# Weight halves that start at changing offsets of 0 to 60 bytes in their buffers

## The chip, the core and the metric

The kernel runs on one core of a Trainium2 chip. The metric is the device time of one execution in microseconds (us). Engine names are those of the profile: PE is the matrix engine, PEld its weight loads, DVE the vector engine, ACT the scalar engine, POOL the general one, SP the queue that issues most DMAs.

## The reference, cut to what matters

Two decoder layers on 256 tokens of width 2048. Each layer projects the normalised input by one wide matrix, feeds four branches (a state-space scan, two attentions, a gated linear attention), projects each branch, gates and sums them, and projects the sum once more. All of it is float32.

```python
h = rmsnorm(x, pre_norm)
proj = h @ w_in                                  # 2048 x 20080 per layer
...                                              # four branches A, B, C, D
mixed = sum(gates[b] * (out[b] @ w_branch[b]) for b in "ABCD")
x = x + rmsnorm(mixed @ w_out, post_norm)
```

Weights are read once: 455 MB in all.

## The kernel before, in words

**Pieces of weight.** The weights are laid out on the host as pieces of 128 partitions x 1024 words (512 KB). `fetch` (L154 to L161) brings one piece: an SP DMA into a `raw` tile (five buffers), then ACT rounds it into `hi` (L158, an F32R tile, the matrix engine's rounded form of a 4-byte float), and DVE writes the rest `raw - hi` into `lo` (L159). `hi` and `lo` have three buffers each. 842 pieces go this way; six more, in the last stage of each layer, use buffers of their own (`own`, rows named `w_last`).

**Three products instead of one.** An activation is kept as two halves too (`hh`, `hl` in the tile `hx`; `oX_h`, `oX_l` of a branch X; `m_h`, `m_l`). A product is `hi*hh + lo*hh + hi*hl`.

- `chunk_a` (L165): the weight piece is the *moving* operand, 512 columns at a time; the activation is the stationary one, loaded anew for each matmul. A piece serves 12 matmuls of 512 columns (2 blocks of K, 2 halves of the tokens, 3 products), L179, L180, L181. 674 of the 842 pieces are used so.
- `chunk_b` (L186): the weight piece is the *stationary* operand, 128 columns at a time, and the activations move past it. A piece serves 8 loads of `hi` with 512 moving columns (L196, L200) and 8 loads of `lo` with 256 (L198). 144 pieces.
- `chunk_b4` (L213, 20 pieces) and the small projections (4 pieces of 896 words) also load the piece as stationary.

**Order.** The chunks run in a fixed order, layer by layer: acc_c, small, acc_lg, acc_uq/ur/uk/uv, acc_g, acc_gv, acc_gg, then for D, C, A and B a merge (acc_mX: gate, acc_bX: branch projection), between them acc_x, acc_z, acc_f, acc_fv, acc_fg, and acc_y last. The branch computations are generators that are stepped once per piece (`step`), so their instructions lie between the pieces' matmuls.

**Where the buffers lie.** In the built program the three `hi` buffers start 4096 bytes apart in each partition, the three `lo` buffers and the five `raw` buffers likewise, each on a multiple of 64 bytes. A matmul takes its columns from a `hi` or `lo` buffer from word 0 on in steps of 128, 256 or 512 words (112 words in the small projections), so every read of a piece starts on a multiple of 64 bytes.

Of the kernel before, what the change touches and what calls it, by code (L numbers as in the profile page):

```python
# [10 lines left out]
F32R = mybir.dt.float32r  # L11
# [7 lines left out]
P = 128  # L19
# [18 lines left out]
def trunk(ctx: ExitStack, tc: tile.TileContext, x, pos, vecs, rows, dskip, pre, post, glaw2,  # L38
# [5 lines left out]
    st = ctx.enter_context(tc.tile_pool(name="st", bufs=1))  # L44
# [96 lines left out]
    def step(n=1):  # L141
        for _ in range(n):
            while bg:
                try:
                    next(bg[0])
                    break
                except StopIteration:
                    bg.pop(0)

    def drain(gen=None):  # L150
        while bg and (gen is None or gen in bg):
            step()

    def fetch(src, n=1024, own=None):  # L154
        raw = st.tile([P, 1024], F32, tag="raw", name="raw", bufs=5)
        nc.sync.dma_start(raw[:, :n], src)
        hi, lo = own or (st.tile([P, 1024], F32R, tag=t, name=t, bufs=3) for t in ("hi", "lo"))
        S.copy(hi[:, :n], raw[:, :n])  # L158
        V.tensor_tensor(lo[:, :n], raw[:, :n], hi[:, :n].bitcast(F32), ALU.subtract)  # L159
        return hi, lo  # L160
# [4 lines left out]
    def chunk_a(src, p0, nk, xh, xl, k0, name, groups=None, own=None):  # L165

        acc = acc_tile(name)
        a2 = [acc[:, 0], acc[:, 1]]
        if own:
            a2[1] = ps.tile([P, 2, 512], F32, tag="s", name=name + "_1")[:, 0]  # L170
        kp = 0
        for n in groups or [1] * (nk // 2):
            w = [fetch(src[p0 + kp + i], own=own[i] if own and n > 1 else None) for i in range(n)]
            ks = [(2 * kp + i, w[i // 2], slice((i % 2) * 512, (i % 2 + 1) * 512)) for i in range(2 * n)]
            order = ([(tt, k) for k in ks for tt in range(2)] if n == 1 else
                     [(tt, k) for tt in range(2) for k in ks])
            for tt, (k, (hi, lo), c) in order:
                ts_ = slice(tt * P, (tt + 1) * P)
                PE.matmul(a2[tt], xh[:, k0 + k, ts_], hi[:, c], start=(k == 0), stop=False)  # L179
                PE.matmul(a2[tt], xh[:, k0 + k, ts_], lo[:, c], start=False, stop=False)  # L180
                PE.matmul(a2[tt], xl[:, k0 + k, ts_], hi[:, c], start=False, stop=(k == nk - 1))  # L181
            kp += n
            step(n)
        return a2 if own else acc

    def chunk_b(src, p0, name):  # L186

        acc = acc_tile(name)
        for b in range(2):
            for kh in range(2):  # L190
                hi, lo = fetch(src[p0 + 2 * b + kh])
                for k8 in range(8):
                    k = kh * 8 + k8
                    c = slice(k8 * P, (k8 + 1) * P)
                    if k < 15:
                        PE.matmul(acc[:, b], hi[:, c], hx[:, k].rearrange("p a t -> p (a t)"),  # L196
                                  start=(k == 0), stop=False)
                    PE.matmul(acc[:, b, 0:T], lo[:, c], hh[:, k], start=False, stop=False)  # L198
                    if k == 15:
                        PE.matmul(acc[:, b], hi[:, c], hx[:, k].rearrange("p a t -> p (a t)"),  # L200
                                  start=False, stop=True)
                step()
        return acc.rearrange("p b (a t) -> p b a t", a=2)
# [9 lines left out]
    def chunk_b4(src, p0, nb, xh, xl, k0, name):  # L213
        acc = acc_tile(name).rearrange("p a (b t) -> p (a b) t", t=T)
        for pp in range(nb // 2):
            hi, lo = fetch(src[p0 + pp])
            for j in range(2):
                b = 2 * pp + j
                for k in range(4):
                    c = slice((j * 4 + k) * P, (j * 4 + k + 1) * P)  # L220
                    PE.matmul(acc[:, b], hi[:, c], xh[:, k0 + k], start=(k == 0), stop=False)
                    PE.matmul(acc[:, b], hi[:, c], xl[:, k0 + k], start=False, stop=False)
                    PE.matmul(acc[:, b], lo[:, c], xh[:, k0 + k], start=False, stop=(k == 3))
            step()
        return acc
# [135 lines left out]
    for l in range(DEPTH):  # L361
# [27 lines left out]
        for kh in range(2):  # L389
            hi, lo = fetch(w_sm[l, kh], 896)  # L390
# [460 lines left out]
        for c in range(4):  # L851
            own = None
            if c == 3:
                own = sl.tile([P, 4, 1024], F32R, tag="mixed", name="w_last0")
                own2 = slot(7, "w_last1", F32R).rearrange("p (a n) -> p a n", a=2)
                own = [(own[:, 0], own[:, 1]), (own[:, 2], own[:, 3]), (own2[:, 0], own2[:, 1])]
# [114 lines left out]
```

## Time and profile before

| | |
|---|---|
| median of the runs | 2578.92 us (2578.37 to 2579.47, 2 runs) |
| profiled execution | 2579.64 us, its span 2577.6 us, so 2.0 us around the span |
| PE / PEld | 2546.1 / 2145.5 us busy (99% / 83%) |
| DVE / ACT | 1550.0 / 1259.8 us busy (60% / 49%) |
| HBM | 455 MB read, 178 GB/s over the span |
| granted clock of PE | 0.998 |

A row of the groups reads: line, engine, operation, out<-in, shapes, count | busy us, mean ns | idle time before it and what ended it. The ends of matmuls in the profile are modelled, so two rows of PE overlap (a mean of 390 ns where the next one starts 0.23 us later); the pace of PE is read from the starts.

### The profile page before, as it was taken

The numbers are of one execution on the slowest core, as the hardware profiler recorded it, in microseconds if no ns is written. First come the engines' busy times: TensorE is split into PE (matmuls) and PEld (weight loads), VectorE is DVE, ScalarE is ACT, GpSimd is POOL, SyncE is SP. The second block draws the span as 40 slices with busy tenths as digits, with TensorE's granted clock in tenths as the row PEclk, the third lists the DMA queues.
The fourth block names the chain that finished last, engine by engine and source line by source line (L and its number), as shares of the span: only waits on it lengthen the run. The fifth ranks groups of instructions, "written<-read, shape, count | busy, mean of one in ns | idle before, by whom it ended". The sixth has DMA issues, their size and how long they took to land.

```text
span 2577.6 us, 32544 instructions
## 1 busy us (share of the span) xinstructions
PE 2546.1 (99%) x12658; PEld 2145.5 (83%) x12658; DVE 1550.0 (60%) x1928; ACT 1259.8 (49%) x1625; POOL 25.6 (1%) x33
## 2 busy tenths in 40 slices
PE   8999999999999999999989999999999999999998
PEld 6898888888888888888878888888888888888887
DVE  6755855766655555555567568547665555565555
ACT  5554544555444444444455455445554454444443
POOL 0000000000000000000000000000000000000000
PEclk9999999999999999999999999999999999999999
DMA  6554555555555555665655445555555555556654
GB/s 227 182 164 147 168 168 183 185 180 171 193 183 180 172 172 186 206 189 180 211 163 187 156 146 168 171 185 187 176 172 191 188 177 173 173 172 204 189 180 155
DMA packets 126715, 461.34 MB, mean 179 GB/s; under 512 B 14657, under 2 KB 15169, under 8 KB 125665
## 3 DMA queue, kind: packets, MB, share of 16 engines
q1 hardware_dynamic: 126144, 459.11, 55.0%
q8 instruction: 99, 1.62, 0.3%
q14 instruction: 56, 0.45, 0.1%
q10 hardware_dynamic: 416, 0.17, 0.0%
HBM read 455.02 MB, written 4.19 MB: 178 GB/s over the span
## 4 chain that ended last, share of the span: by engine, by line
PE 98%; DVE 1%; ACT 1%; issue 0%; DMA 0%; POOL 0%; SPq 0%; DVEq 0%; POOLq 0%; ACTq 0%
PE acc_f L196 4%; PE acc_x L196 3%; PE acc_f L198 2%; PE acc_mC L180 2%; PE acc_mA L180 2%; PE acc_mA L179 2%; PE acc_mD L180 2%; PE acc_mC L179 2%; PE acc_mA L181 2%; PE acc_mD L179 2%; PE acc_mC L181 2%; PE acc_mD L181 2%; PE acc_mB L180 2%; PE acc_mB L179 2%; PE acc_mB L181 2%; PE acc_g L196 2%
## 5 line engine op out<-in xcount | busy, mean ns | idle before, releaser
L159 DVE TENSOR_TENSOR lo<-raw,hi 128x1024 fp32r<-128x1024 f32 x842 | 1027.9, 1223 | 796.1 <-ACT hi L158 793.7
L158 ACT CAST hi<-raw 128x1024 fp32r<-128x1024 f32 x842 | 883.4, 1050 | 1034.3 <-PE acc_mB L181 93.6
L196 PE MATMUL acc_f<-hx,hi 128*128 128x512 f32 x480 | 170.9, 397 | 0.0
L198 PE MATMUL acc_f<-hx,lo 128*128 128x256 f32 x512 | 139.7, 283 | 0.0
L196 PE MATMUL acc_x<-hx,hi 128*128 128x512 f32 x360 | 128.0, 396 | 0.0
L196 PEld LDWEIGHTS acc_f<-hx,hi 128*128 128x128 f32 x480 | 90.2, 188 | 20.1
L198 PE MATMUL acc_x<-hx,lo 128*128 128x256 f32 x384 | 105.0, 284 | 0.0
L180 PE MATMUL acc_mA<-lo,hx 128*128 128x512 f32 x256 | 103.7, 405 | 0.0
L180 PE MATMUL acc_mC<-lo,hx 128*128 128x512 f32 x256 | 102.7, 401 | 0.0
L180 PE MATMUL acc_mD<-lo,hx 128*128 128x512 f32 x256 | 102.4, 400 | 0.0
L179 PE MATMUL acc_mA<-hi,hx 128*128 128x512 f32 x256 | 101.6, 397 | 0.0
L181 PE MATMUL acc_mA<-hi,hx 128*128 128x512 f32 x256 | 100.5, 393 | 0.0
L179 PE MATMUL acc_mC<-hi,hx 128*128 128x512 f32 x256 | 100.3, 392 | 0.0
L180 PE MATMUL acc_mB<-lo,hx 128*128 128x512 f32 x256 | 100.2, 391 | 0.0
L179 PE MATMUL acc_mD<-hi,hx 128*128 128x512 f32 x256 | 99.9, 390 | 0.0
L181 PE MATMUL acc_mD<-hi,hx 128*128 128x512 f32 x256 | 99.8, 390 | 0.0
L181 PE MATMUL acc_mC<-hi,hx 128*128 128x512 f32 x256 | 99.7, 389 | 0.0
L181 PE MATMUL acc_mB<-hi,hx 128*128 128x512 f32 x256 | 99.7, 389 | 0.0
L179 PE MATMUL acc_mB<-hi,hx 128*128 128x512 f32 x256 | 99.6, 389 | 0.0
L198 PEld LDWEIGHTS acc_f<-hx,lo 128*128 128x128 f32 x512 | 96.6, 189 | 3.0
L181 PE MATMUL acc_y<-hi,m_l 128*128 128x512 f32 x232 | 91.5, 394 | 0.0
L180 PE MATMUL acc_y<-lo,m_h 128*128 128x512 f32 x232 | 90.4, 390 | 0.0
(422 smaller groups left out, 5637.7 us busy)
## 6 DMA issues: line engine op xcount, KB each, us to landing
raw<-in_w_in_dram SPq DMA_DIRECT2D x624, 512.0 KB, 3.4
raw<-in_w_br_dram SPq DMA_DIRECT2D x128, 512.0 KB, 3.4
raw<-in_w_out_dram SPq DMA_DIRECT2D x64, 512.0 KB, 4.0
raw<-in_w_ukv_dram SPq DMA_DIRECT2D x16, 512.0 KB, 4.3
raw<-in_w_uq_dram SPq DMA_DIRECT2D x12, 512.0 KB, 3.5
x<-in_x_dram SPq DMA_DIRECT2D x4, 512.0 KB, 5.6
xr<-in_x_dram SPq DMA_DIRECT2D x2, 1024.0 KB, 5.7
pn<-in_post_dram SPq DMA_DIRECT2D x2, 1024.0 KB, 5.5
```

What stands on the lines that cost most here:

```text
L158: S.copy(hi[:, :n], raw[:, :n])
L159: V.tensor_tensor(lo[:, :n], raw[:, :n], hi[:, :n].bitcast(F32), ALU.subtract)
L179: PE.matmul(a2[tt], xh[:, k0 + k, ts_], hi[:, c], start=(k == 0), stop=False)
L180: PE.matmul(a2[tt], xh[:, k0 + k, ts_], lo[:, c], start=False, stop=False)
L181: PE.matmul(a2[tt], xl[:, k0 + k, ts_], hi[:, c], start=False, stop=(k == nk - 1))
L196: PE.matmul(acc[:, b], hi[:, c], hx[:, k].rearrange("p a t -> p (a t)"), start=(k == 0), stop=False)
L198: PE.matmul(acc[:, b, 0:T], lo[:, c], hh[:, k], start=False, stop=False)
```

## The change

`fetch` takes `hi` and `lo` from buffers of 1040 words instead of 1024, and uses 1024 words of them that begin at word `i % 16` (for `hi`) and `(i + i // 16) % 16` (for `lo`), where `i` counts the pieces. So the start moves by 4 bytes from piece to piece, over 0 to 60 bytes, and the distance between the two starts changes every 16 pieces. The six pieces with buffers of their own stay as they were.

```diff
+    nth = [0]
+
     def fetch(src, n=1024, own=None):
         raw = st.tile([P, 1024], F32, tag="raw", name="raw", bufs=5)
         nc.sync.dma_start(raw[:, :n], src)
-        hi, lo = own or (st.tile([P, 1024], F32R, tag=t, name=t, bufs=3) for t in ("hi", "lo"))
+        if own:
+            hi, lo = own
+        else:
+            i = nth[0]
+            nth[0] += 1
+            hi, lo = (st.tile([P, 1040], F32R, tag=t, name=t, bufs=3)[:, o:o + 1024]
+                      for t, o in (("hi", i % 16), ("lo", (i + i // 16) % 16)))
         S.copy(hi[:, :n], raw[:, :n])
         V.tensor_tensor(lo[:, :n], raw[:, :n], hi[:, :n].bitcast(F32), ALU.subtract)
         return hi, lo
```

In the built program the instructions of every engine stand in the same order as before, row for row (11,670 rows on PE, 1,627 on DVE, 1,383 on ACT, 38 on POOL, 873 on SP), on the same buffers. What differs is addresses. The three `hi` buffers, and the three `lo` buffers, lie 4160 bytes apart instead of 4096, and all tiles behind them move up by a multiple of 64 bytes (384 bytes behind the last). Of the 8,088 matmuls with a piece as moving operand, 4,048 now start at an odd word and 6,060 at an address that is no multiple of 16 bytes; of the 2,880 loads of a piece as stationary operand, 1,432 and 2,160.

## The prediction

> **What bounds the kernel now.** I read the page's head first, then the chain that ended last, the groups, and the waits around `fetch`.
>
> ```profile
> span 2577.6 us, 32544 instructions
> PE 2546.1 (99%) x12658; PEld 2145.5 (83%) x12658; DVE 1550.0 (60%) x1928; ACT 1259.8 (49%) x1625; POOL 25.6 (1%) x33
> PE   8999999999999999999989999999999999999998
> PEclk9999999999999999999999999999999999999999
> PE 98%; DVE 1%; ACT 1%; issue 0%; DMA 0%; POOL 0%; SPq 0%; DVEq 0%; POOLq 0%; ACTq 0%
> ```
>
> PE is busy in every slice at full granted clock, and 98% of the chain is PE's own instructions, one after the other. So the time is the sum of PE's paces, and a change counts only if it alters the pace of a matmul or makes PE wait. Does PE wait for the split of a weight piece, the only code that the diff touches? The answers for the lines L159 and L158 list who waited for them:
>
> ```profile
>   ACT hi L158: 793.7, 619
>   PEld acc_c L180: 1.0, 2
>   PE acc_c L180: 0.4, 1
> ...
>   PEld acc_c L179: 3.5, 1
>   PE acc_c L179: 3.1, 1
> ```
>
> DVE waits 619 times for ACT's rounding (793.7 us), but PE waited for `lo` or `hi` only in acc_c, the first chunk, a few us in all. The split runs ahead. How far, and at what pace PE goes meanwhile, shows in the timeline of a merge stage:
>
> ```profile
> 1102.70 0.39 PE L180 MATMUL acc_mB<-lo,hx 128*128 128x512 f32 x1
> 1102.93 0.39 PE L181 MATMUL acc_mB<-hi,hx 128*128 128x512 f32 x1
> 1103.15 0.39 PE L179 MATMUL acc_mB<-hi,hx 128*128 128x512 f32 x1
> 1103.35 1.05 ACT L158 CAST hi<-raw 128x1024 fp32r<-128x1024 f32 x1 [1.66 <-PE acc_mB L181]
> 1103.38 0.39 PE L180 MATMUL acc_mB<-lo,hx 128*128 128x512 f32 x1
> 1103.61 0.39 PE L181 MATMUL acc_mB<-hi,hx 128*128 128x512 f32 x1
> ...
> 1104.44 1.22 DVE L159 TENSOR_TENSOR lo<-raw,hi 128x1024 fp32r<-128x1024 f32 x1 [1.49 <-ACT hi L158]
> ...
> 1105.65 0.39 PE L181 MATMUL acc_mB<-hi,hx 128*128 128x512 f32 x1
> ...
> 1106.07 1.05 ACT L158 CAST hi<-raw 128x1024 fp32r<-128x1024 f32 x1 [1.67 <-PE acc_mB L181]
> ```
>
> From the L181 at 1102.93 to the one at 1105.65 are 12 matmuls in 2.72 us: a start every 227 ns, 2.72 us per `chunk_a` piece. ACT begins a piece when PE frees its buffer (1103.35), DVE ends it at 1105.66, 2.31 us later; with three buffers PE still has two pieces to go, so it wants this one at about 1103.35 + 5.44 = 1108.8. The split is 3.1 us early, more than its own length.
>
> **The change part by part.** No instruction is added, removed or moved, and no wait is added: every engine's order is the same. SP's DMAs fill `raw`, which keeps its form. Four things read or write at new addresses.
>
> *1. ACT writes `hi`, DVE reads `hi` and writes `lo`, 842 times each, at 4 to 60 bytes past a 64-byte boundary in 15 of 16 cases.*
>
> ```profile
> L159 DVE TENSOR_TENSOR lo<-raw,hi 128x1024 fp32r<-128x1024 f32 x842 | 1027.9, 1223 | 796.1 <-ACT hi L158 793.7
> L158 ACT CAST hi<-raw 128x1024 fp32r<-128x1024 f32 x842 | 883.4, 1050 | 1034.3 <-PE acc_mB L181 93.6
> L690 DVE SCALAR_TENSOR_TENSOR xsT<-gt,vec,xsT x48: 475/479/482, 478.0 to 1797.0; 128x255 f32<-128x255 f32 x16, 128x254 f32<-128x254 f32 x16, 128x253 f32<-128x253 f32 x16
> L578 DVE TENSOR_SCALAR gla_x<-glz,vec x8: 475/478/484, 245.6 to 1531.2; 128x256 f32<-128x256 f32 x8
> ```
>
> The convolution (L690, `dst[:, j, i:]` with i of 1 to 3) already has DVE read and write at 4, 8 and 12 bytes: 479 ns for 253 to 255 elements, against 478 for 256 at an aligned place (L578). So DVE's price is 0, within 2 ns. For ACT no row shows such a write; DVE's 0 is the nearest, and the far end is a doubling. Neither end reaches PE alone: twice 1.05 us adds 1.05 to a chain that is 3.1 us early, and ACT's sum would go from 1260 to 2143 us of 2578. I take 0. Below 0 nothing is to be had, because PE does not wait there.
>
> *2. PE streams 8,088 matmuls of 512 columns (674 pieces x 12) from shifted places.* No row shows an F32R moving operand that starts off a 64-byte boundary, so I bound it by the nearest rows: DVE's 0 +/- 2 ns above, and the loads of L269, whose stationary operand `id2[:, 16 + h]` is F32R and starts at 4-byte steps (one word repeated):
>
> ```profile
> L269 PEld LDWEIGHTS S_B<-fR,id x32: 187/189/190, 690.6 to 2289.2; 128*128 128x128 f32 x32
> L198 PEld LDWEIGHTS acc_f<-hx,lo 128*128 128x128 f32 x512 | 96.6, 189 | 3.0
> L196 PEld LDWEIGHTS acc_f<-hx,hi 128*128 128x128 f32 x480 | 90.2, 188 | 20.1
> ```
>
> Across all 16 starts they take 187 to 190 ns, like the aligned loads of L196 and L198. So my value is 0 per matmul and the bounds are -2 and +2 ns: 8,088 x 2 ns = 16 us either way. Nothing covers this term: each ns per matmul is 8 us of time.
>
> [...]
>
> *3. PE loads 2,880 stationary blocks (144 pieces x 16 and the 20 + 4 others) from shifted places.* L269 says 0 +/- 2 ns. The loads run beside matmuls of the block before; uncovered, 2 ns each would be 6 us.
>
> *4. The tiles behind the buffers move by multiples of 64 bytes.* Their accesses keep their place within 64 bytes; I cost that at 0.
>
> Sum: 2579.6 (this execution) + 0, with -22 to +22. The profiled execution lies 0.7 us above the median, so the forecast is **2580 us**.
>
> **The rivals.**
>
> *A. The shift separates accesses that collide (faster).* Before, the buffers of one kind stand 4096 bytes apart, so ACT and DVE write at the offsets at which PE reads. If that cost PE time, matmuls beside a write should be slower, and stages should differ:
>
> ```profile
> L180 PE MATMUL acc_mA<-lo,hx 128*128 128x512 f32 x256 | 103.7, 405 | 0.0
> L180 PE MATMUL acc_mC<-lo,hx 128*128 128x512 f32 x256 | 102.7, 401 | 0.0
> L180 PE MATMUL acc_mD<-lo,hx 128*128 128x512 f32 x256 | 102.4, 400 | 0.0
> L179 PE MATMUL acc_mA<-hi,hx 128*128 128x512 f32 x256 | 101.6, 397 | 0.0
> L181 PE MATMUL acc_mA<-hi,hx 128*128 128x512 f32 x256 | 100.5, 393 | 0.0
> L179 PE MATMUL acc_mC<-hi,hx 128*128 128x512 f32 x256 | 100.3, 392 | 0.0
> L180 PE MATMUL acc_mB<-lo,hx 128*128 128x512 f32 x256 | 100.2, 391 | 0.0
> L179 PE MATMUL acc_mD<-hi,hx 128*128 128x512 f32 x256 | 99.9, 390 | 0.0
> L181 PE MATMUL acc_mD<-hi,hx 128*128 128x512 f32 x256 | 99.8, 390 | 0.0
> L181 PE MATMUL acc_mC<-hi,hx 128*128 128x512 f32 x256 | 99.7, 389 | 0.0
> L181 PE MATMUL acc_mB<-hi,hx 128*128 128x512 f32 x256 | 99.7, 389 | 0.0
> L179 PE MATMUL acc_mB<-hi,hx 128*128 128x512 f32 x256 | 99.6, 389 | 0.0
> ```
>
> The mean of the twelve is 393.8 ns, 4.8 above the lowest. If the whole excess were collisions, 8,088 x 4.8 = 39 us would go: 2541 us, still under 2%. But acc_mB, at the floor, has the same splits beside it as the others; it lacks branch work between its matmuls. And in the timeline the starts come 0.22 to 0.23 us apart whether a cast runs beside them (1103.38 to 1103.61) or neither engine writes (1102.70 to 1102.93). A whole collision relief is unlikely.
>
> *B. PE streams at half its pace from an odd word (slower).* The chain shows that this engine has two paces for 4-byte words: the F32R product of L179 and, beside it, the plain F32 scores of L272, with as many passes of 128 as of 256 columns:
>
> ```profile
> 149.35 0.23 PE acc_uv L179
> 149.58 1.97 PE S_D L272 x12
> ```
>
> 1.97 us / 12 = 164 ns for 192 columns on average, 0.855 ns a column; F32R goes at 227 / 512 = 0.443. If the fast pace needs words taken in pairs from an even place, the 4,048 matmuls that start at an odd word would take 512 x 0.855 = 438 ns, 211 more: 854 us, 3434 us in all. It decides the result from 52 us / 4,048 = 13 ns per odd matmul on. For it: the fast pace is twice the plain one, so something is widened. Against it: L269 and L690, which though repeat one word or take one at a time; no fast stream is among them. This is the rival I can least exclude.
>
> *C. The split itself slows and becomes the bound (slower).* If ACT and DVE both took twice as long off their boundaries, DVE's sum would be 1550 + 1028 = 2578 us, the whole span, and DVE's waits outside the split (2577.6 - 1550.0 - 796.1 = 231 us) would come on top in part: 2578 to 2809 us. It decides as soon as DVE's L159 is slower by some 80%. L690 speaks against it.
>
> **How the numbers follow.** The forecast (every pace within 2 ns) gets 0.80, the page's line penalty 0.05 (2591), rival A 0.04 (down to 2541), rival B 0.08 (3434, or a part of it), rival C 0.02; 0.01 for a gain beyond A. A measurement of this kernel tells about 2% from no change, 52 us. So faster 0.01, same 0.89, slower 0.10. The range takes the bounds of the forecast and the line penalty, which hold 0.85: 2560 to 2602 us. A part of A reaches into it.
>
> **What would show it.** Right: starts in acc_mB every 227 ns at every offset, L159 at 1223 ns and L158 at 1050, PE busy 99%, no wait of PE on `hi` or `lo` outside acc_c. [...] B: pieces alternate, every second one at up to 438 ns a matmul where `hi` starts odd, and acc_f, where pieces are stationary, changes otherwise. C: DVE near 100% and PE waiting for `lo`. What makes the prediction wrong is B first: a fast stream that no row here shows from an odd place.

## The result, and the profile after

The changed kernel takes 2614.44 us (median of 2614.19 to 2614.69) against 2578.92: a ratio of 1.0138, 95% interval 1.0094 to 1.0181. The profiled execution took 2614.69 us, its span is 35.0 us longer than before. The head of its page and its chain:

```profile
span 2612.6 us, 32544 instructions
PE 2580.4 (99%) x12658; PEld 2150.8 (82%) x12658; DVE 1551.8 (59%) x1928; ACT 1257.6 (48%) x1625; POOL 25.6 (1%) x33
PEclk9999999999999999999999999999999999999999
PE 97%; DVE 1%; ACT 1%; issue 0%; DMA 0%; POOL 0%; SPq 0%; DVEq 0%; POOLq 0%; ACTq 0%
```

PE's busy time grew by 34.3 us, so the time is PE's own; its granted clock is 0.997 against 0.998 before, and the waits on the split (DVE's `lo` at L167, ACT's `hi` at L166) are the same few in acc_c:

```profile
  PEld acc_c L188: 1.0, 2
  PE acc_c L188: 0.4, 1
...
  PEld acc_c L187: 3.7, 1
  PE acc_c L187: 3.3, 1
```

The groups say which matmuls (lines are 8 higher than before, 180 is now 188):

```profile
L167 DVE TENSOR_TENSOR lo<-raw,hi 128x1024 fp32r<-128x1024 f32 x842 | 1029.0, 1224 | 823.6 <-ACT hi L166 822.5
L166 ACT CAST hi<-raw 128x1024 fp32r<-128x1024 f32 x842 | 881.0, 1048 | 1070.1 <-PE acc_mB L189 97.9
L204 PE MATMUL acc_f<-hx,hi 128*128 128x512 f32 x480 | 170.4, 395 | 0.0
L206 PE MATMUL acc_f<-hx,lo 128*128 128x256 f32 x512 | 139.8, 283 | 0.0
L188 PE MATMUL acc_mB<-lo,hx 128*128 128x512 f32 x256 | 101.5, 396 | 0.0
L187 PE MATMUL acc_mB<-hi,hx 128*128 128x512 f32 x256 | 101.0, 395 | 0.0
L189 PE MATMUL acc_mB<-hi,hx 128*128 128x512 f32 x256 | 101.0, 395 | 0.0
```

Casts and subtractions are unchanged (1224 and 1048 ns against 1223 and 1050). `chunk_b`, where the piece is stationary, is unchanged (395 and 283 against 397 and 283; a pair of one matmul with `hi` and one with `lo` takes 350.6 ns from start to start in both). `chunk_a` is slower everywhere: the rows of acc_mB go from 389 to 391 up to 395 and 396. In the timeline of that stage:

```profile
1114.01 0.39 PE L189 MATMUL acc_mB<-hi,hx 128*128 128x512 f32 x1
1114.24 0.40 PE L187 MATMUL acc_mB<-hi,hx 128*128 128x512 f32 x1
1114.48 0.40 PE L188 MATMUL acc_mB<-lo,hx 128*128 128x512 f32 x1
...
1116.79 0.40 PE L189 MATMUL acc_mB<-hi,hx 128*128 128x512 f32 x1
```

From 1114.01 to 1116.79 are 12 starts: 232 ns each, against 227. Over all `chunk_a` matmuls that follow directly on one another, the mean distance of starts in the trace is 228.1 ns before and 232.7 after; 4.6 x 8,088 = 37 us, so these matmuls account for the whole loss of 35. Sorted by the word at which the moving half begins, the mean is 235 ns for words 1, 5, 9, 13, 233 for 2, 6, 10, 14, 231 for 3, 7, 11, 15, and 232 for 0, 4, 8, 12. So there is a saw-tooth over 16 bytes, and under it a rise that aligned starts pay too (232 at words 0, 4, 8, 12 against the 228.1 of before).

### The profile page after: what moved, and what is told of

It reads as the page before. It is cut to its first block, busy times and chain, and to the rows that moved or that the text cites. A ratio compares the mean times of both kernels' runs of the same rounds, so it can differ in the third digit from the quotient of the medians.

```text
span 2612.6 us, 32544 instructions
## 1 busy us (share of the span) xinstructions
PE 2580.4 (99%) x12658; PEld 2150.8 (82%) x12658; DVE 1551.8 (59%) x1928; ACT 1257.6 (48%) x1625; POOL 25.6 (1%) x33
## 4 chain that ended last, share of the span: by engine, by line
PE 97%; DVE 1%; ACT 1%; issue 0%; DMA 0%; POOL 0%; SPq 0%; DVEq 0%; POOLq 0%; ACTq 0%
PE acc_f L204 4%; PE acc_x L204 3%; PE acc_mC L188 2%; PE acc_mA L188 2%; PE acc_f L206 2%; PE acc_mD L188 2%; PE acc_mA L189 2%; PE acc_mA L187 2%; PE acc_mC L187 2%; PE acc_mD L187 2%; PE acc_mB L187 2%; PE acc_mB L189 2%; PE acc_mC L189 2%; PE acc_mB L188 2%; PE acc_mD L189 2%; PE acc_y L189 2%
## 5 line engine op out<-in xcount | busy, mean ns | idle before, releaser
L167 DVE TENSOR_TENSOR lo<-raw,hi 128x1024 fp32r<-128x1024 f32 x842 | 1029.0, 1224 | 823.6 <-ACT hi L166 822.5
L166 ACT CAST hi<-raw 128x1024 fp32r<-128x1024 f32 x842 | 881.0, 1048 | 1070.1 <-PE acc_mB L189 97.9
```

## The experiments

All times below are medians, beside runs of the kernel before on the same chip (2578.6 to 2579.5). "Pace" is the mean distance between the starts of `chunk_a` matmuls that follow directly on one another, worked out from the starts in the trace (distances over 270 ns, next to branch matmuls, are left out); acc_mB and acc_bB are the quietest stages, acc_mA has branch work between its matmuls.

| run | time, us | ratio (95%) | acc_mB | acc_bB | acc_mA |
|---|---|---|---|---|---|
| before | 2578.92 | | 226.9 | 226.7 | 229.3 |
| after | 2614.44 | 1.0138 (1.0094 to 1.0181) | 232.6 | 232.5 | 233.0 |
| pad_only | 2602.10 | 1.0089 (1.0074 to 1.0104) | 231.5 | 231.9 | 231.3 |
| const1 | 2649.27 | 1.0272 (1.0257 to 1.0287) | 237.5 | 237.7 | 237.2 |
| const3 | 2590.52 | 1.0044 (1.0029 to 1.0059) | 229.4 | 229.5 | 230.0 |
| lines | 2604.39 | 1.0098 (1.0081 to 1.0115) | 231.7 | 231.5 | 231.7 |
| both64 | 2590.42 | 1.0043 (1.0028 to 1.0058) | 229.0 | 228.9 | 230.0 |
| lo64 | 2608.39 | 1.0112 (1.0097 to 1.0127) | 231.9 | 232.0 | 231.9 |
| all64 | 2578.95 | 0.9999 (0.9989 to 1.0008) | 226.8 | 226.7 | 229.2 |
| hx15 | 2601.32 | 1.0084 (1.0069 to 1.0099) | 228.9 | 226.7 | 233.0 |
| sweep64 | 2600.31 | 1.0083 (1.0063 to 1.0104) | by chunk | | |
| sweep4 | 2611.28 | 1.0126 (1.0106 to 1.0146) | by chunk | | |
| sweep_lo | 2597.58 | 1.0073 (1.0053 to 1.0093) | by chunk | | |
| all4b | 2660.61 | 1.0316 (1.0299 to 1.0334) | 237.7 | 236.7 | 237.6 |
| frame | 2579.21 | 1.0000 (0.9991 to 1.0010) | 226.9 | 226.7 | 229.3 |
| word7 | 2572.95 | 0.9979 (0.9970 to 0.9988) | 227.2 | 227.2 | 227.5 |
| word7_b | 2573.07 | 0.9977 (0.9968 to 0.9987) | 227.2 | 227.2 | 227.5 |

### Place, mixing or spacing

Four kernels keep the 1040-word buffers and replace the two offsets of the change:

```diff
-                      for t, o in (("hi", i % 16), ("lo", (i + i // 16) % 16)))
+                      for t, o in (("hi", 0), ("lo", 0)))                              # pad_only
+                      for t, o in (("hi", 1), ("lo", 1)))                              # const1
+                      for t, o in (("hi", 3), ("lo", 3)))                              # const3
+                      for t, o in (("hi", 4 * (i % 4)), ("lo", 4 * ((i + i // 4) % 4))))  # lines
```

**pad_only**

> Buffers of 1040 words, every half begins at word 0. In the changed kernel a chunk_a matmul starts on average 4.3 ns later after the one before it, 35 us over 8,088 of them. Three theories. Place: it costs where a moving operand begins within 16 bytes (in the trace after, matmuls from words 1, 5, 9, 13 take about 235 ns to the next start, from 2, 6, 10, 14 about 233, from the others about 231). Mixing: it costs that neighbouring matmuls begin at different places, so that the even pace of 227 ns is lost. Spacing: it costs that the buffers stand 4160 bytes apart and other tiles moved. Place and mixing expect the time before, 2579 us; spacing expects about 2614.

**const1**

> All halves begin at word 1 of buffers of 1040 words. Place: the dearest place, without the aligned ones between; the one merge piece after the change with both halves at word 1 went at 238 ns a matmul against 227 before: 11 x 8,088 = 89 us, about 2668 us; at the least the 4 ns that separate words 1 and 0 in the trace after, 2611. Mixing: all starts are alike, so the even pace returns: 2579. Spacing: about 2614, as with word 0.

**const3**

> All halves begin at word 3 of buffers of 1040 words. Place: 228 to 230 ns a matmul, as in the merge pieces after the change with both halves at word 3, 7 or 15: 2587 to 2603 us, far below word 1 though the address is as odd. Mixing: 2579. Spacing: about 2614.

**lines**

> Starts change from piece to piece, but only by multiples of 16 bytes: word 4*(i%4) for hi and 4*((i+i//4)%4) for lo. [...] Mixing: neighbours still begin at different addresses, so the aligned matmuls pay what they pay in the trace after (231.5 ns against 228.1 before between such starts): 3.4 x 8,088 = 27 us, 2606. Spacing: about 2614.

Measured: pad_only loses 23 us with every start on a multiple of 64 bytes. That is 64% of the change's loss without its offsets, which "place" and "mixing" did not expect; "spacing" expected the whole. const1 is 47 us slower than pad_only, const3 12 us faster, so there is a place effect on top, and it is not oddness (237.5 ns at word 1, 229.4 at word 3 in acc_mB). The two parts do not simply add: at word 3 these buffers cost half of what they cost at word 0. "Mixing" falls with pad_only, const1 and const3, whose starts are all alike and which it put at 2579. lines does not decide against it: its 2604 us lie near the 2606 of "mixing", and 2 us above pad_only, so starts that change by multiples of 16 bytes cost next to nothing over the spacing.

Does the spacing act through ACT and DVE, which write beside PE? In acc_mB of pad_only the same 12 distances (ns) return whenever the same pair of buffers comes round. Two passes of one pair, worked out from the starts; A or D marks a distance of which ACT or DVE was busy for more than half:

```
231   240A  230A  234A  231A  232D  233D  240D  230D  234D  231D  232
231   240AD 230AD 234AD 231AD 232D  233D  240D  230D  234D  231D  232D
```

The pattern is the same, whatever the writers do (away from branch matmuls, over all passes, within 1 to 2 ns wherever a distance was seen with and without a writer). Over acc_mB and acc_bB the mean is 232.3 with neither busy, 231.3 with ACT, 231.7 with DVE, 231.1 with both. So no collision with the writers shows in these stages; what is left to look at is the addresses that PE itself reads, and the next runs move those.

### Which addresses

```diff
+            V.memset(st.tile([P, 16], F32, tag="gap_hi", name="gap_hi"), 0.0)   # both64: once, ahead of hi
             hi = st.tile([P, 1024], F32R, tag="hi", name="hi", bufs=3)
+            V.memset(st.tile([P, 16], F32, tag="gap_lo", name="gap_lo"), 0.0)   # lo64: once, ahead of lo
             lo = st.tile([P, 1024], F32R, tag="lo", name="lo", bufs=3)
+    V.memset(cp.tile([P, 16], F32, tag="gap_hx", name="gap_hx"), 0.0)           # all64: ahead of hx
-    hx = cp.tile([P, 16, 2, T], F32R, tag="hx", name="hx")                      # hx15, then rearranged to the four axes
+    hx = cp.tile([P, 16 * 2 * T + 16], F32R, tag="hx", name="hx")[:, 15:15 + 16 * 2 * T]
```

**both64**

> Buffers of 1024 words as before, 4096 bytes apart, but a gap of 64 bytes stands before the hi buffers, so all halves lie 64 bytes higher against the activations (hx, and the branch halves). Three theories for the 23 us that buffers of 1040 words cost with every start at word 0. Activations: PE's pace depends on where the moving half lies against the stationary block that is loaded for the next matmul; before, both are equal modulo 512 bytes, here they differ by 64: slower than 2579, towards the 2602 of the 1040-word buffers. Halves: it depends on where hi lies against lo (192 bytes apart modulo 512 in the 1040-word buffers, 0 here): 2579. Absolute: some addresses are slow in themselves: slower, like the first.

**lo64**

> As before, but a gap of 64 bytes between the hi and the lo buffers: hi stays equal to hx modulo 512 bytes, lo lies 64 higher. Activations: only the matmuls with lo (one in three) change their place against the stationary block: about a third of what all halves moved by 64 bytes cost. Halves: hi and lo differ in every piece: the full cost, towards 2602.

**all64**

> As before, but a gap of 64 bytes stands before hx, so that activations and halves all move up by 64 bytes together. Activations and halves: every relation is as before, 2579. Absolute: as slow as with the halves alone moved by 64 bytes.

**hx15**

> The activations hx begin at word 15 of a buffer that is 16 words longer; the halves of the weights start at word 0 of buffers of 1024 words. Seen from hx the halves lie 4 bytes further, as they did with all halves at word 1; the branch halves lie 64 bytes higher and keep their relation to the weights. If the dear places within 16 bytes (word 1) are places against the stationary block, the chunk_a stages with hx (acc_m, acc_gv, acc_fv and so on) go at 235 to 238 ns, as with all halves at word 1, and the time is near 2640. If they are places of the moving operand by itself, those stages go at 227 to 232 ns and only chunk_b, where hx moves, can change. acc_bX and acc_y, whose stationary blocks are not in hx, stay at 227 to 229 either way.

Measured: all64 returns to 2579 and to the paces of before, so 64 bytes more on every address cost nothing; only distances count at that step. both64 pays 11 us (229.0 ns in acc_mB against 226.9): the distance from the moving halves to the stationary blocks counts. lo64 pays 29 us, in all three products alike (232), though `hi` kept its distance to `hx`: the distance between `hi` and `lo`, which follow each other as moving operands, counts too, and more. Both theories of a distance hold in part; "a third of the cost" for lo64 was a miss.

hx15 was unclear on its own: the stages with `hx` go at 229 to 234, the branch stages as before, so there is a distance effect, but not the 237 of const1. In acc_mB the trace holds two even rhythms at the same distances, 226 and 227 ns in some stretches, 233 and 234 in others. The first chunk has both:

```profile
1074.54 0.39 PE L179 MATMUL acc_mB<-hi,hx 128*128 128x512 f32 x1
1079.98 0.40 PE L179 MATMUL acc_mB<-hi,hx 128*128 128x512 f32 x1
1080.21 1.04 PE L233 MATMUL tr_oB<-ident,fg 128*128 128x128 f32 x8
1081.32 0.39 PE L181 MATMUL acc_mB<-hi,hx 128*128 128x512 f32 x1
1097.41 0.40 PE L181 MATMUL acc_mB<-hi,hx 128*128 128x512 f32 x1
```

The first 24 distances are 226.7 ns on average, then eight branch matmuls come in, and the 69 distances from 1081.32 on are 233.2. The two last acc_mB chunks of the layer, with no branch matmul among theirs, keep 226.7 throughout. So one set of distances allows more than one pace (226.7 and 233.2 ns); in the first chunk the change stands at the branch matmuls.

### The law, by chunk

The sweeps use buffers of 1152 words (4608 bytes apart, equal modulo 512 again), four `raw` buffers instead of five to make room, and one offset per `chunk_a` chunk; everything else stays at word 0:

```diff
+        hi, lo = (st.tile([P, 1152], F32R, tag=t, name=t, bufs=3)[:, o:o + 1024]
+                  for t, o in (("hi", place[0]), ("lo", place[1])))
...
+        place[:] = 16 * (c % 8), 16 * (c % 8)                            # sweep64, c-th chunk_a
+        place[:] = (c + 4 * (c // 52)) % 16, (c + 4 * (c // 52)) % 16    # sweep4
+        place[:] = 0, 16 * (c % 8)                                       # sweep_lo
+        place[:] = 1, 1                                                  # all4b, with hx from word 1 of a longer buffer
```

**sweep64**

> Buffers of 1152 words (4608 bytes apart, equal modulo 512 as before; raw has four buffers instead of five). Every chunk_a chunk uses one distance for both halves, 64*(c mod 8) bytes for the c-th chunk, so the halves lie 0, 64, ... 448 bytes from the stationary blocks modulo 512 and equal to each other. Relation theory (the pace follows the distance between moving half and stationary block): the chunks at 0 go at 227 ns, those at 64 at 229 as in the run with all halves moved by 64 bytes, the others at paces of their own between 225 and 236, the same in both layers. If only the distance between hi and lo counts, all go at 227 to 229.

The timeline of sweep64, first and last start of an undisturbed row of matmuls in four neighbouring chunks, with both halves 256, 320, 384 and 448 bytes (0, 64, 128 and 192 modulo 256) from the stationary blocks; 95, 47, 95 and 47 distances lie between:

```profile
1139.83 0.39 PE L188 MATMUL acc_mB<-hi,hx 128*128 128x512 f32 x1
1161.40 0.39 PE L190 MATMUL acc_mB<-hi,hx 128*128 128x512 f32 x1
1161.63 0.40 PE L188 MATMUL acc_bB<-hi,oB_h 128*128 128x512 f32 x1
1172.40 0.39 PE L190 MATMUL acc_bB<-hi,oB_l 128*128 128x512 f32 x1
1172.63 0.40 PE L188 MATMUL acc_mB<-hi,hx 128*128 128x512 f32 x1
1194.72 0.39 PE L190 MATMUL acc_mB<-hi,hx 128*128 128x512 f32 x1
1194.95 0.39 PE L188 MATMUL acc_bB<-hi,oB_h 128*128 128x512 f32 x1
1205.91 0.40 PE L190 MATMUL acc_bB<-hi,oB_l 128*128 128x512 f32 x1
```

That is 227.1, 229.1, 232.5 and 233.2 ns. The chunks of the same stages one layer later, at 0, 64, 128 and 192, go at 227.1, 229.3, 232.5 and 233.2: the pattern repeats every 256 bytes.

**sweep_lo**

> The same buffers; hi stays at word 0, lo alone lies 64*(c mod 8) bytes higher. With lo 64 bytes higher in the earlier run every matmul took 232 ns, more than with both halves 64 higher (229). If the distance between hi and lo has its own price, the chunks at 0 go at 227 and all seven others at 230 to 234; if only the matmuls with lo pay by their distance to the stationary block, the chunk means lie a third of the way that the chunks with both halves moved go.

The same four distances for `lo` alone:

```profile
1137.58 0.39 PE L188 MATMUL acc_mB<-hi,hx 128*128 128x512 f32 x1
1159.16 0.39 PE L190 MATMUL acc_mB<-hi,hx 128*128 128x512 f32 x1
1159.38 0.39 PE L188 MATMUL acc_bB<-hi,oB_h 128*128 128x512 f32 x1
1170.29 0.40 PE L190 MATMUL acc_bB<-hi,oB_l 128*128 128x512 f32 x1
1170.53 0.39 PE L188 MATMUL acc_mB<-hi,hx 128*128 128x512 f32 x1
1192.68 0.39 PE L190 MATMUL acc_mB<-hi,hx 128*128 128x512 f32 x1
1192.91 0.40 PE L188 MATMUL acc_bB<-hi,oB_h 128*128 128x512 f32 x1
1203.68 0.39 PE L190 MATMUL acc_bB<-hi,oB_l 128*128 128x512 f32 x1
```

227.2, 232.1, 233.2 and 229.1 ns: at 64 bytes dearer than with both halves moved, at 192 cheaper. The distance between the halves has its own price (232.1 ns against 229.1 at 64 bytes). The expectation missed one thing: not all seven other distances are dear, since 256 bytes (227.2 ns) cost as little as 0 does in sweep64 (227.1). And the pace is not fixed by the distances alone: with `lo` 128 bytes (modulo 256) higher, undisturbed chunks of acc_lg and acc_y go at 231.1 ns, beside the 233.2 of acc_mB.

This also reads pad_only. There a third of the pieces have `hi` at distance 0 and `lo` 192 bytes higher (in the built program the three `hi` buffers lie 0, 64 and 128 bytes from `hx` modulo 256, the `lo` buffers 192, 0 and 64). Within such a piece of acc_bB the distances are 228 to 230 ns, as the 229.1 here, but for one of 240 after its first matmul, behind a piece of another buffer.

**sweep4**

> The same buffers, but both halves of a chunk begin at word 0, 1, ... 15, by chunk. If the place within 16 bytes has a price of its own, words 1, 5, 9, 13 are 4 to 10 ns dearer than words 0, 4, 8, 12, and words 2, 6, 10, 14 half as much; words 3, 7, 11, 15 cost about what 0, 4, 8, 12 do. If the dear places came only from buffers that stand 4160 bytes apart, all 16 go within 2 ns.

Quiet chunks at words 0, 1, 3, 5, 6 and 7 in the timeline of sweep4 (69, 47, 47, 47, 95 and 47 distances):

```profile
2379.03 0.39 PE L190 MATMUL acc_mB<-hi,hx 128*128 128x512 f32 x1
2394.70 0.39 PE L190 MATMUL acc_mB<-hi,hx 128*128 128x512 f32 x1
2394.92 0.40 PE L188 MATMUL acc_bB<-hi,oB_h 128*128 128x512 f32 x1
2406.10 0.40 PE L190 MATMUL acc_bB<-hi,oB_l 128*128 128x512 f32 x1
2429.63 0.39 PE L188 MATMUL acc_bB<-hi,oB_h 128*128 128x512 f32 x1
2440.39 0.39 PE L190 MATMUL acc_bB<-hi,oB_l 128*128 128x512 f32 x1
2462.85 0.40 PE L188 MATMUL acc_bB<-hi,oB_h 128*128 128x512 f32 x1
2474.05 0.40 PE L190 MATMUL acc_bB<-hi,oB_l 128*128 128x512 f32 x1
2474.29 0.40 PE L188 MATMUL acc_mB<-hi,hx 128*128 128x512 f32 x1
2496.47 0.40 PE L190 MATMUL acc_mB<-hi,hx 128*128 128x512 f32 x1
2496.70 0.40 PE L188 MATMUL acc_bB<-hi,oB_h 128*128 128x512 f32 x1
2507.39 0.39 PE L190 MATMUL acc_bB<-hi,oB_l 128*128 128x512 f32 x1
```

227.1, 237.9, 228.9, 238.3, 233.5 and 227.4 ns. All sixteen words, each the mean of its acc_mB or acc_bB chunks:

| word | 0 | 1 | 2 | 3 | 4 | 5 | 6 | 7 | 8 | 9 | 10 | 11 | 12 | 13 | 14 | 15 |
|---|---|---|---|---|---|---|---|---|---|---|---|---|---|---|---|---|
| ns | 227.2 | 237.8 | 233.5 | 229.0 | 231.6 | 238.3 | 233.5 | 227.4 | 233.2 | 234.8 | 233.4 | 230.0 | 233.3 | 233.9 | 232.3 | 227.3 |

Their mean is 232.3, near the pace of the changed kernel in acc_mB (232.6); since its halves lie at other distances from each other, that may be chance. Words 1, 5, 9, 13 are the dearest of each four and word 3, 7, 11, 15 the cheapest or near it, as expected. But words 4, 8, 12 cost 4.4 to 6.1 ns over word 0, which the place theory did not expect: they are distances of 16, 32 and 48 bytes. So words 9 and 13 are only 1.6 and 0.6 ns dearer than the aligned words beside them, and place and distance are mixed in this table.

**all4b**

> The same buffers; all halves of chunk_a begin at word 1 and the activations hx too, so in the stages with hx (acc_m, acc_gv, acc_z and so on) the distances are 0 again and only the place within 16 bytes is odd. In acc_bX, acc_uv and acc_y the stationary blocks start at a multiple of 64 bytes, 4 bytes from the halves. Relation theory: the hx stages return to 227 to 229 ns, the others are slow. Place theory: hx stages and the others alike are 4 to 10 ns slower than 227, 2611 to 2660 us in all.

Here is the group of rows that separates place from distance at word 1: acc_mB, where halves and `hx` both begin at word 1.

```profile
1165.67 0.40 PE L188 MATMUL acc_mB<-hi,hx 128*128 128x512 f32 x1
1188.26 0.40 PE L190 MATMUL acc_mB<-hi,hx 128*128 128x512 f32 x1
```

95 distances of 237.8 ns, as at word 1 against aligned blocks. So what word 1 costs (237.8 ns against 227.2 at word 0) belongs to the moving operand's own place, and not to its distance from the blocks; for the other words no run separates the two. `chunk_b` agrees: in this run `hx` moves there from word 1, and the pair of one 512-column and one 256-column matmul goes from 350.6 ns before to 358.9.

### The frame, and a faster kernel

**frame** (all at word 0)

> The frame of the sweeps alone: buffers of 1152 words, four raw buffers, every half at word 0. Distances modulo 512 as before. If the frame is neutral: 2579 us, chunk_a paces as before (227 quiet, 228 to 229 busy). If spacing 4608 or the fourth raw buffer costs: above 2590.

**word7** (`place[:] = 7, 7` in `chunk_a`)

> The same frame, all chunk_a halves at word 7 (28 bytes). From the sweep by words: quiet stages 227.2 as at word 0, busy ones 227.4 against 229.0 at word 0; so 0 to 1.6 ns x 8,088 less than the frame: 2566 to 2579 us. If the dear pace comes from being off 16 bytes as such, or if the sweep's chunks were fast only by their neighbours: 2600 or more.

**word7_b** (word7, and in `chunk_b` and `chunk_b4` by chunk)

> As word7, and chunk_b takes its pieces (stationary) at words 0, 16, 32, 48, 3, 7, 11, 15, 1 by chunk, chunk_b4 at 0, 16, 32, 48, 7. If the stationary operand's place costs by itself like the moving one's, the chunks at word 1 are 4 to 10 ns a matmul dearer; if only distances count for it, they differ by 0 to 6 ns in no order of words; the time stays within 10 us of word7, since chunk_b is 2,304 of the loads.

Measured: the frame is neutral (1.0000). word7, whose every moving half is off 16 and off 8 bytes, is *faster* than before: 2572.95 us, 0.9979 (0.9970 to 0.9988). The quiet stages lose 0.3 to 0.5 ns a matmul, the busy ones gain, as the groups of acc_mA of frame (first row) and word7 show:

```profile
L188 PE MATMUL acc_mA<-hi,hx 128*128 128x512 f32 x256 | 101.6, 397 | 0.0
```

```profile
L188 PE MATMUL acc_mA<-hi,hx 128*128 128x512 f32 x256 | 100.8, 394 | 0.0
```

At word 0 the distances of acc_mA spread from 224 to 236 ns between its branch matmuls (229.3 on average); at word 7 most stay at 226 to 228 (227.5 on average). That is the first kernel here that beats the one before.

word7_b is equal to word7. In its `chunk_b` chunks a pair takes 350.2 ns with the stationary piece at word 0, 350.5 at word 1, 350.1 at 3, 353.0 at 7, 347.2 at 11, 362.4 at 15, and 351.2 to 352.2 at 64 to 192 bytes. Aligned `chunk_b` chunks of the frame already differ by 348 to 353 ns, so nothing can be read from a few ns here. Word 1 is not dear: the 10.6 ns that it costs a moving operand do not show for a stationary one (350.5 against 350.2 ns a pair). Word 15 does stand out, by 12 ns a pair against the expected 0 to 6, and why stays open.

## Why the prediction was wrong

*Where the bound lies* held: PE alone sets the time (busy 99% before and after), and the loss is a pace of PE (228.1 to 232.7 ns), not a wait. That the loss stayed under the 2% of the forecast is luck: two of the four terms failed, and const1, with one fixed odd place, lost 2.7%.

*Step 1 (ACT and DVE, 0)* held: 1048 and 1224 ns. The convolution's rows were the right witness for DVE.

*Step 2 (8,088 matmuls, 0 with bounds of -2 and +2 ns)* is one of the two terms that failed. It measured +4.6 ns on average, of which aligned starts in the longer buffers already pay 3.3 (pad_only, 231.4 against 228.1), and between 0 and 11 ns by place (sweep4, 227.2 to 238.3). The bounds came from DVE's L690 and from the loads of L269. Neither is a fast stream of moving columns: all4b and word7_b show that the same word 1 costs 11 ns a matmul in `chunk_a` and 8 ns a pair in `chunk_b` where the operand moves, and 0.3 ns a pair where it is stationary. The text said that no row shows such a stream, and still set the bounds as if the nearest rows were near.

*Step 3 (2,880 loads, 0)* held: `chunk_b` rows are within 2 ns of before, and its pairs at 350.6 ns.

*Step 4 (tiles that move by multiples of 64 bytes, 0)* failed, and its failure is the larger part. It took every shift by a multiple of 64 bytes as free and looked only at the tiles behind; that the `hi` and `lo` buffers themselves now stand 64 bytes further each, and `lo` 192 bytes (modulo 512) from `hi`, was no term of the sum. pad_only makes these shifts alone and loses 23 of the 35 us; both64 (+11 us), lo64 (+29) and all64 (0) show that it is the distances between PE's operands that cost.

The range also ended 2 us short below (2580 - 22 is 2558, not 2560), which changes nothing here.

*Rival A* was right that distances between buffers count, and had the wrong partner and sign. Distances do cost, but between the operands that PE reads (lo64, 231.9 ns in acc_mB); the equal spacing of before was the good case (226.9), and the writers made no difference where pad_only was looked at (231.1 to 232.3 with and without them). *Rival B* saw that the moving stream was the unknown, but the price is not a half pace (211 ns) and not oddness: word 1 costs 10.6 ns, words 7 and 15 0.2 or less (sweep4: 237.8, 227.4 and 227.3 against 227.2). *Rival C* did not occur: DVE is busy 59%, its L167 takes 1224 ns.

*The line penalty* that the chances and the range name (2591 us, 11 above the forecast) is a term that no run shows. In its place the runs showed a price that goes by the word: in sweep4 word 1 costs 10.6 ns over word 0 and word 7 costs 0.2, though both are off 16 bytes. The changed kernel loses 12.3 us over pad_only, near those 11, which looks like chance, for one price for every start off 16 bytes would put words 1 and 7 at the same pace.

What stays open is the mechanism. The runs show what the pace of quiet stages depends on (the word at which the moving operand begins; distances modulo 256 bytes between moving halves and stationary blocks, and between the halves), but no formula: one set of distances holds two paces (226.7 and 233.2 ns in hx15, 231.1 and 233.2 in sweep_lo). They don't show what in the memory or in PE makes it so.

## What to carry to other kernels

PE is busy 99% of the time here, and the addresses of its operands move the time: these runs lie between 0.2% faster (word7) and 3.2% slower (all4b) than before. A good first choice, by these runs, is equal addresses modulo 256 bytes for the moving tiles that follow each other and the stationary blocks loaded beside them (227 ns in sweep64, against 229 to 233 at 64 to 192 bytes), and a buffer's size is not to be changed by a few words without a look at the distance of starts in a quiet stage. An aligned start was not enough here (pad_only, 2602.10 us), and an unaligned one was not slow as such (word 7, 28 bytes off, was the fastest kernel, 2572.95 us). When a resource has no row in the trace, its bounds must come from a row of the same kind of access, or stay wide.

## What the runs showed of the hardware that was not expected

- PE's pace for 512-column F32R matmuls with a new stationary block each was 227 ns at distance 0 and 229, 232.5 and 233 at 64, 128 and 192 bytes between the moving halves (both moved alike) and the stationary blocks, and the same at 256 bytes more (sweep64, quiet stages).
- Moving halves that begin at word 1, 5, 9 or 13 cost 7 to 11 ns a matmul over word 0, at word 3, 7, 11 or 15 0 to 3 (sweep4, distances included); at word 1 the 10.6 ns stay where the distance to the blocks is 0 (all4b). A stationary operand at word 1 shows no such cost: 350.5 ns a pair against 350.2 at word 0 (word7_b).
- The time from one matmul's start to the next was the same within 1 to 2 ns whether ACT and DVE wrote or not: 232.3 ns with neither busy, 231.3 with ACT, 231.7 with DVE, 231.1 with both (pad_only, acc_mB and acc_bB).
- At one set of distances PE kept two even rhythms, 226.7 and 233.2 ns (hx15); in the chunk shown the switch stands at eight branch matmuls.
